# Joint gated norms, two banks for the turned chunks, two banks for the keys' products

## The chip, the cores and the metric

The kernel runs on one core of a Trainium2 chip. The core has five engines that run side by side and are ordered only by semaphores: TensorE (matrix products, results into the accumulator memory PSUM), VectorE, ScalarE, GpSimd and SyncE, which here issues the transfers. The metric is the device time of one execution in microseconds; lower is better. All data are float32. A product of two float32 matrices of full precision is made of three products of split operands (high by high, high by low, low by high), the lines L191 to L193.

## The reference, cut to what matters

One layer of a diffusion backbone over 1024 latent tokens and 256 context tokens, width 1024: a token mixer and then a convolutional channel mixer. The change lies in the token mixer, in its gated-DeltaNet heads (4 heads of 128):

```python
def bidir_gdn(q, k, v, beta, g, s0_f, s0_b):
    o_f, s_f = gated_delta_chunked(q, k, v, beta[:, :, 0], g[:, :, 0], s0_f)
    o_b, s_b = gated_delta_chunked(flip(q), flip(k), flip(v), flip(beta[:, :, 1]), flip(g[:, :, 1]), s0_b)
    return o_f + flip(o_b), s_f, s_b
...
kb = kc * bc[..., None]
a_mat = jnp.where(strict, jnp.einsum('nbhid,nbhjd->nbhij', kb, kc) * decay, 0.0)
t_inv = lax.linalg.triangular_solve(eye + a_mat, ...)   # per chunk and head
...
def mixer_out(u, o, z, w_f, g_gdn_l, w_out_l):
    y_f = fourier_mix(u, w_f)
    y_d = rmsnorm(o, g_gdn_l) * jax.nn.silu(z).reshape(...)
    return jnp.concatenate([y_f, y_d.reshape(bsz, length, V_W)], axis=-1) @ w_out_l
```

So each chunk needs the keys' products with themselves (`kc` with `kc`), times a decay, inverted; two scans run over the chunks in opposite directions; their sum is normalised per token and head (the norm), multiplied by a gate (gated norm), and goes with the Fourier part through the output projection.

## The kernel before, in words

Tokens are cut into ten tiles of 128: two of context, eight latent ones. The program is written as generators that are interleaved by hand (`both` alternates several, `drive` puts projection work between the yields of a main chain); a scheduler then lays out each engine's instructions in one fixed order. In a run each engine works through its own order and waits at its head.

The chain goes by batches of tiles. `decays` makes, per tile and direction, a decay matrix: two small rows are turned (L925), cast by ScalarE (L927), spread by GpSimd (L929, the tile `rh`), multiplied on TensorE (L953, L954) and exponentiated by ScalarE (L955). Once per tile, for both directions, TensorE makes the keys' products (L943, four heads) in the bank `sb`; VectorE multiplies them by the decay (L956), once per direction. Between them `lanes` of the batch before runs on VectorE: 31 steps of a product and a subtraction (L983, L985) on all triangles at once. Its result goes through DRAM (L988, L990), GpSimd masks it (L1007), and TensorE uses it (`finish`, L1013). Beside it TensorE has projections (L191 to L193) with convolutions on VectorE (L716 to L718, L735 on ScalarE).

Then ten scan steps follow, each on a pair of tiles, one per direction (`scan_step`). GpSimd scales a copy of the keys (L1102, `kd`), TensorE's products are all recorded at L1082, and VectorE updates the state (L1144) and the output (L1131, L1150). In the steps 6 to 9 both tiles of a step are finished for both directions (`seen`). Then each is normalised (`gdn_scale`): squares and sums on ScalarE (L1164), eight small instructions of VectorE on 128x4 values, among them the reciprocal square root of L201 to L206 (its root, L202, is ScalarE's), and four scalings of 128x128 on VectorE (L1170). One step later `gdn_out` turns each with four transposes (L1180) into a bank of the tag `a`, of which there is one; VectorE multiplies by the gate (L1182), ScalarE casts (L1189) and GpSimd takes the low part (L165). L165 is a helper: all subtractions for split operands carry that line. The banks have tags: `mm` has two, `g` three, `a` one, `sf` and `sb` one each; the scan uses `sf` and `sb` for its two directions.

The projection of the mixer's output runs over two groups of four tiles, in two halves of columns (`first_half`, `second_half`). It needs the turned chunks and the Fourier pages, which `load_yf` brings from DRAM (cast at L1204, split at L165). The norm behind it is L1365 and L1366. From about 660 us on the channel mixer runs; the change does not touch it.

Of the kernel before, what the change touches and what calls it, by code (L numbers as in the profile page):

```python
# [9 lines left out]
F32 = mybir.dt.float32  # L10
F32R = mybir.dt.float32r
BF16 = mybir.dt.bfloat16
AF = mybir.ActivationFunctionType
ALU = mybir.AluOpType
# [4 lines left out]
P = 128  # L19
# [5 lines left out]
NTC = CTX // P  # L25
NTA = NT + NTC
H = 4
# [73 lines left out]
class Kern:  # L101
# [802 lines left out]
    def decays(self, B):  # L904

        nc, kp, tiles = self.nc, self.kp, B["tiles"]
        V = nc.vector
# [28 lines left out]
        for u, (ti, t, d) in enumerate(units):  # L936
            st, rh = nxt
            if u + 1 < nu:
                nxt = rows(*units[u + 1][1:])
            if d == 0:  # L940
                kk = self.psum("sb")
                for h in range(H):
                    nc.tensor.matmul(kk[:, h * P:(h + 1) * P], self.kchunk(h, t), self.kchunk(h, t),  # L943
                                     start=True, stop=True, skip_group_check=True)
                W2 = self.pg().rearrange("p (d h n) -> p d h n", d=2, h=H)
                if t >= NTC:
                    EP = self.pg()
                    E2 = EP[:, 0:512], EP[:, 512:]
            W = W2[:, d]
            W = W.rearrange("p h n -> p (h n)")  # L950
            e = E2[d] if t >= NTC else W
            ps = self.psum("g")
            nc.tensor.matmul(ps, self.negm[:, d], self.idb.rearrange("p h n -> p (h n)"), start=True, stop=False)  # L953
            nc.tensor.matmul(ps, st[:, 0], rh.rearrange("p h n -> p (h n)"), start=False, stop=True)  # L954
            nc.scalar.activation(e, ps, AF.Exp)  # L955
            V.tensor_tensor(W, kk, e, op=ALU.mult)  # L956
            W = W2[:, d]
            for b in range(4):
                s = slice(32 * b, 32 * b + 32)
                (V.transpose if d == 0 else nc.scalar.copy)(CB[s, u], W[s, :, s])  # L960
            if d:
                nc.sync.dma_start(B["dw"][ti], W2.rearrange("p d h n -> p d (h n)"))
                if t >= NTC:
                    nc.sync.dma_start(self.Ed[t], EP.rearrange("p (d n) -> p d n", d=2))
            yield 1
# [97 lines left out]
    def scan_step(self, si):  # L1063

        nc = self.nc
        V = nc.vector
# [6 lines left out]
        R, vt, E, kd, vs, qs, o = ([None, None] for _ in range(7))  # L1073
        S = self.S
        T = self.steps[si]
# [14 lines left out]
        for d in range(2):  # L1090
            t = T[d]
# [54 lines left out]
        if lat:  # L1146
            for d in range(2):
                av = self.psum("g")
                mm(av, lambda h: E[d][:, hs(h)], lambda h: vs[d][:, hs(h)])
                V.tensor_tensor(o[d], o[d], av, op=ALU.add)  # L1150
            if seen:
                for d in range(2):
                    self.gdn_scale(T[d] - NTC)
        yield 1

    def gdn_scale(self, lt):

        nc, sp = self.nc, self.kp
        V = nc.vector
        o = self.o[lt]  # L1160
        ss = sp.tile([P, 2, H], F32, tag="oss", bufs=2, name=self.nm("oss"))
        s = self.sq[:, lt]
        for h in range(H):
            nc.scalar.activation(self.junk[:, :P], o[:, h * P:(h + 1) * P], AF.Square, accum_out=ss[:, 0, h:h + 1])  # L1164
        V.tensor_tensor(ss[:, 0], ss[:, 0], s, op=ALU.mult)
        V.tensor_tensor(ss[:, 0], ss[:, 0], s, op=ALU.mult)
        self.rsqrt(ss[:, 1], ss[:, 0], 1.0 / P, sp)
        V.tensor_tensor(ss[:, 1], ss[:, 1], s, op=ALU.mult)
        for h in range(H):
            V.tensor_scalar_mul(o[:, h * P:(h + 1) * P], o[:, h * P:(h + 1) * P], ss[:, 1, h:h + 1])  # L1170

    def gdn_out(self, lt):

        nc = self.nc
        o = self.o[lt]
        z = self.pg()[:, 0:512].rearrange("p (h n) -> p h n", h=H)
        nc.sync.dma_start(z, self.zs[:, :, lt * P:(lt + 1) * P].rearrange("h p n -> p h n"))
        ps = self.psum("a")
        for h in range(H):
            nc.tensor.transpose(ps[:, h * P:(h + 1) * P], o[:, h * P:(h + 1) * P], self.ident)  # L1180
        zf = z.rearrange("p h n -> p (h n)")
        nc.vector.scalar_tensor_tensor(zf, ps, self.gg, zf, op0=ALU.mult, op1=ALU.mult)  # L1182
        g, c0 = GCOL[lt]
        if self.yT[g][4] is None:
            self.yT[g][4:] = [self.page2() for _ in range(4)]
        for h in range(H):
            y = self.yT[g][4 + h]
            c = slice(c0, c0 + P)
            nc.scalar.copy(y[:, 0, c], z[:, h])  # L1189
            self.sub_l(nc.gpsimd, y[:, 1, c], z[:, h], y[:, 0, c])  # L1190
# [16 lines left out]
    def mixer(self):  # L1207
# [6 lines left out]
        with tc.tile_pool(name="mix", bufs=1, reuse_waits="tile") as kp:  # L1214
# [30 lines left out]
            for si in range(6, 10):  # L1245
# [6 lines left out]
                next(g)  # L1252
                if si >= 8:
                    next(h00)
                for lt in late:
                    self.gdn_out(lt)
                if si == 11:
                    self.load_yf(1)
                if si == 10:
# [15 lines left out]
            h10 = self.second_half(0, gp)  # L1275
            for _ in range(2):
                next(h10)
            for lt in late:
                self.gdn_out(lt)
            if 11 == 11:  # L1280
                self.load_yf(1)
            x0, self.h0w = [], []
# [590 lines left out]
```

## Time and profile before

| | |
|---|---|
| three runs | 1362.92, 1364.43, 1364.84 us (median 1364.43) |
| profiled execution | 1366.19 us, its span 1364.4 |
| TensorE busy | 1285.0 us (94% of the span) |
| VectorE busy | 992.6 us (73%) |
| ScalarE, GpSimd busy | 641.1 us (47%), 472.2 us (35%) |
| chain that ended last | TensorE 56%, VectorE 22%, DMA 8%, issue 5%, ScalarE 5% |

Busy shares are means over stages with different limits. In the rows below PE is TensorE's products, PEld its weight loads, DVE VectorE, ACT ScalarE, POOL GpSimd. "idle before <-releaser" is how long the engine stood still before an instruction and what it waited for. PEclk is the share of TensorE's full clock that was granted, as a mean over the window. One product of float32 shows as several records on TensorE, so four of them read "x8".

### The profile page before, as it was taken

The numbers are of one execution on the slowest core, as the hardware profiler recorded it, in microseconds if no ns is written. First come the engines' busy times: TensorE is split into PE (matmuls) and PEld (weight loads), VectorE is DVE, ScalarE is ACT, GpSimd is POOL, SyncE is SP. The second block draws the span as 40 slices with busy tenths as digits, with TensorE's granted clock in tenths as the row PEclk, the third lists the DMA queues.
The fourth block names the chain that finished last, engine by engine and source line by source line (L and its number), as shares of the span: only waits on it lengthen the run. The fifth ranks groups of instructions, "written<-read, shape, count | busy, mean of one in ns | idle before, by whom it ended". The sixth has DMA issues, their size and how long they took to land.

```text
span 1364.4 us, 19307 instructions
## 1 busy us (share of the span) xinstructions
PE 1285.0 (94%) x6678; PEld 1025.0 (75%) x6678; DVE 992.6 (73%) x1802; ACT 641.1 (47%) x1334; POOL 472.2 (35%) x464
## 2 busy tenths in 40 slices
PE   5999999989899999898999899999999999999994
PEld 2677886667557789786777688888888887888873
DVE  2465555944963856857469899888888889878997
ACT  5553456532554233444757444444444445555342
POOL 0221114332434252542126667665666650000000
PEclk9999999999999999999999899999999999999997
DMA  9622226676476778825432233332233166645665
GB/s 333 179 107 71 74 77 193 209 220 209 150 201 236 273 229 275 269 64 172 163 131 79 77 94 93 93 93 66 59 92 93 47 208 231 201 137 165 201 216 185
DMA packets 183732, 213.67 MB, mean 157 GB/s; under 512 B 31640, under 2 KB 119762, under 8 KB 183634
## 3 DMA queue, kind: packets, MB, share of 16 engines
q1 hardware_dynamic: 182769, 209.28, 47.8%
q0 software_dynamic: 864, 3.15, 0.7%
q8 instruction: 53, 0.87, 0.3%
q14 instruction: 46, 0.37, 0.1%
HBM read 163.11 MB, written 49.28 MB: 156 GB/s over the span
## 4 chain that ended last, share of the span: by engine, by line
PE 56%; DVE 22%; DMA 8%; issue 5%; ACT 5%; POOL 2%; SPq 1%; DVEq 0%; POOLq 0%; ACTq 0%
PE ps L191 14%; PE ps L193 14%; PE ps L192 14%; DVE cv L1472 4%; PE ps L1082 3%; DVE T L983 2%; DVE pg L985 2%; PE ps L305 2%; PE ps L1026 2%; DVE pg L1449 1%; DVE wl L165 1%; DVE pg L165 1%; PE ps L1013 1%; DVE s L1449 1%; DMA pg<-in_x_dram 1%
## 5 line engine op out<-in xcount | busy, mean ns | idle before, releaser
L191 PE MATMUL ps<-pg,wh 128*128 128x512 f32 (+1 forms) x896 | 351.7, 393 | 7.6 <-DVE pad L1449 5.2
L192 PE MATMUL ps<-pg,wh 128*128 128x512 f32 (+1 forms) x896 | 346.2, 386 | 0.0
L193 PE MATMUL ps<-pg,wl 128*128 128x512 f32 (+1 forms) x896 | 346.2, 387 | 0.0
L1472 DVE SCALAR_TENSOR_TENSOR cv<-pad,dw,cv 128x1024 f32<-128x1024 f32 x176 | 226.3, 1286 | 11.6 <-ACT cv L1470 8.2
L191 PEld LDWEIGHTS ps<-pg,wh 128*128 128x128 f32 x896 | 169.8, 190 | 56.1 <-issue 20.7
L193 PEld LDWEIGHTS ps<-pg,wl 128*128 128x128 f32 x896 | 169.7, 189 | 35.7 <-issue 3.5
L192 PEld LDWEIGHTS ps<-pg,wh 128*128 128x128 f32 x896 | 170.2, 190 | 30.9 <-issue 0.4
L165 POOL TENSOR_TENSOR wl<-wr,wh 128x512 fp32r<-128x512 f32 x68 | 89.4, 1322 | 188.7 <-ACT wh L183 158.0
L165 POOL TENSOR_TENSOR wl<-s,wh 128x512 fp32r<-128x512 f32 x80 | 107.7, 1349 | 62.2 <-ACT wh L1651 61.9
L1651 ACT CAST wh<-s 128x512 fp32r<-128x512 f32 x80 | 49.6, 621 | 120.1 <-PE ps L192 116.0
L191 PE MATMUL ps<-pg,pg 128*128 128x512 f32 (+1 forms) x248 | 98.5, 399 | 3.3 <-ACT pg L1616 1.8
L191 PE MATMUL ps<-wh,pg 128*128 128x512 f32 x250 | 97.8, 393 | 2.0 <-ACT pg L1616 1.7
L192 PE MATMUL ps<-pg,pg 128*128 128x512 f32 (+1 forms) x248 | 97.5, 395 | 1.0 <-POOL pg L165 0.7
L193 PE MATMUL ps<-pg,pg 128*128 128x512 f32 (+1 forms) x248 | 96.8, 395 | 1.4 <-DVE pg L355 0.8
L192 PE MATMUL ps<-wl,pg 128*128 128x512 f32 x250 | 97.6, 390 | 0.0
L193 PE MATMUL ps<-wh,pg 128*128 128x512 f32 x250 | 97.3, 390 | 0.0
L1082 PE MATMUL ps<-pg,pg 128*128 128x128 f32 x464 | 58.4, 277 | 0.7 <-ACT pg L1142 0.6
L191 PEld LDWEIGHTS ps<-pg,pg 128*128 128x128 f32 x248 | 47.7, 192 | 14.9 <-ACT pg L1616 2.2
L193 PEld LDWEIGHTS ps<-pg,pg 128*128 128x128 f32 x248 | 47.5, 193 | 13.8 <-issue 1.7
L1082 PEld LDWEIGHTS ps<-pg,pg 128*128 128x128 f32 x464 | 54.9, 192 | 2.7 <-ACT pg L1142 1.0
L192 PEld LDWEIGHTS ps<-pg,pg 128*128 128x128 f32 x248 | 47.8, 193 | 11.2 <-POOL pg L165 1.1
L191 PEld LDWEIGHTS ps<-wh,pg 128*128 128x128 f32 x250 | 46.9, 188 | 12.3 <-ACT pg L1616 2.1
(363 smaller groups left out, 2434.5 us busy)
## 6 DMA issues: line engine op xcount, KB each, us to landing
pg<-in_w_down_dram SPq DMA_DIRECT2D x97, 256.0 KB, 4.5
wr<-in_w_ada_dram SPq DMA_DIRECT2D x32, 512.0 KB, 4.5
wr<-in_w_up_dram SPq DMA_DIRECT2D x24, 512.0 KB, 3.8
wr<-in_w_in_dram SPq DMA_DIRECT2D x20, 512.0 KB, 4.3
pg<-in_w_up_dram SPq DMA_DIRECT2D x20, 512.0 KB, 5.4
wr<-in_w_down_dram SPq DMA_DIRECT2D x35, 256.0 KB, 2.7
gd<-pg SPq DMA_DIRECT2D x17, 512.0 KB, 2.7
pg<-gd SPq DMA_DIRECT2D x34, 256.0 KB, 4.6
```

Source lines behind the costliest of these rows:

```text
L165: eng.tensor_tensor(l, full, h.bitcast(F32), op=ALU.subtract)
L191: nc.tensor.matmul(out, ah, bh, start=start, stop=False, **kw)
L192: nc.tensor.matmul(out, ah, bl, start=False, stop=False, **kw)
L193: nc.tensor.matmul(out, al, bh, start=False, stop=stop, **kw)
L305: nc.tensor.matmul(ps[32 * j:32 * j + 32, :], self.csil[:, k, :], t[:, a, :], start=(k < 4), stop=(k >= 4), skip_group_check=True, tile_po ...
L983: V.tensor_tensor(tmp, L[:nl, j + 1:, j:j + 1].broadcast_to([nl, r, c]), X[:nl, j:j + 1, 0:c].broadcast_to([nl, r, c]), op=ALU.mult)
L985: V.tensor_tensor(X[:nl, j + 1:, 0:c], X[:nl, j + 1:, 0:c], tmp, op=ALU.subtract)
L1026: nc.tensor.matmul(ps[po, h * n:(h + 1) * n], Q[k0:k0 + kn, d, h, po], R[k0:k0 + kn, d, h, c0:c0 + n], start=True, stop=True, skip_group_c ...
L1082: nc.tensor.matmul(ps[:, hs(h)], lhs(h), rhs(h), start=True, stop=True, skip_group_check=True)
L1449: eng.tensor_tensor(o, a, b, op=op)
L1472: V.scalar_tensor_tensor(c3, src, w, c3, op0=ALU.mult, op1=ALU.add)
L1651: nc.scalar.copy(h, src)
```

## The change

Three edits, and the order that the scheduler makes of them. (1) In `decays` the keys' products go to `sb` and `sf` in turn, by the tile's place in its batch. (2) `gdn_scale` takes both tiles of a step: the small instructions are made once, on 128x8 values in place of 128x4 twice, and the scaling of each tile is one VectorE multiply of 128x512 with the factors broadcast over each head's 128 columns (L1173), in place of four of 128x128. The squares on ScalarE stay eight. (3) `gdn_out` takes a tag: the second tile of a step is turned in a bank of `g`. Behind the edited functions the line numbers are three higher: L1180 is L1183, L1182 is L1185.

```diff
--- before.py
+++ after.py
@@ -938,7 +938,7 @@
             if u + 1 < nu:
                 nxt = rows(*units[u + 1][1:])
             if d == 0:
-                kk = self.psum("sb")
+                kk = self.psum(("sb", "sf")[ti % 2])
                 for h in range(H):
                     nc.tensor.matmul(kk[:, h * P:(h + 1) * P], self.kchunk(h, t), self.kchunk(h, t),
                                      start=True, stop=True, skip_group_check=True)
@@ -1149,33 +1149,36 @@
                 mm(av, lambda h: E[d][:, hs(h)], lambda h: vs[d][:, hs(h)])
                 V.tensor_tensor(o[d], o[d], av, op=ALU.add)
             if seen:
-                for d in range(2):
-                    self.gdn_scale(T[d] - NTC)
+                self.gdn_scale([t - NTC for t in T])
         yield 1
 
-    def gdn_scale(self, lt):
+    def gdn_scale(self, lts):
 
         nc, sp = self.nc, self.kp
         V = nc.vector
-        o = self.o[lt]
-        ss = sp.tile([P, 2, H], F32, tag="oss", bufs=2, name=self.nm("oss"))
-        s = self.sq[:, lt]
-        for h in range(H):
-            nc.scalar.activation(self.junk[:, :P], o[:, h * P:(h + 1) * P], AF.Square, accum_out=ss[:, 0, h:h + 1])
+        lts = sorted(lts)
+        ss = sp.tile([P, 2, 2, H], F32, tag="oss", bufs=2, name=self.nm("oss"))
+        s = self.sq[:, lts[0]:lts[1] + 1:lts[1] - lts[0]]
+        for i, lt in enumerate(lts):
+            for h in range(H):
+                nc.scalar.activation(self.junk[:, :P], self.o[lt][:, h * P:(h + 1) * P], AF.Square,
+                                     accum_out=ss[:, 0, i, h:h + 1])
         V.tensor_tensor(ss[:, 0], ss[:, 0], s, op=ALU.mult)
         V.tensor_tensor(ss[:, 0], ss[:, 0], s, op=ALU.mult)
-        self.rsqrt(ss[:, 1], ss[:, 0], 1.0 / P, sp)
+        flat = lambda x: x.rearrange("p a h -> p (a h)")
+        self.rsqrt(flat(ss[:, 1]), flat(ss[:, 0]), 1.0 / P, sp)
         V.tensor_tensor(ss[:, 1], ss[:, 1], s, op=ALU.mult)
-        for h in range(H):
-            V.tensor_scalar_mul(o[:, h * P:(h + 1) * P], o[:, h * P:(h + 1) * P], ss[:, 1, h:h + 1])
-
-    def gdn_out(self, lt):
+        for i, lt in enumerate(lts):
+            o = self.o[lt].rearrange("p (h n) -> p h n", h=H)
+            V.tensor_tensor(o, o, ss[:, 1, i].unsqueeze(2).broadcast_to([P, H, P]), op=ALU.mult)
+
+    def gdn_out(self, lt, tag="a"):
 
         nc = self.nc
         o = self.o[lt]
         z = self.pg()[:, 0:512].rearrange("p (h n) -> p h n", h=H)
         nc.sync.dma_start(z, self.zs[:, :, lt * P:(lt + 1) * P].rearrange("h p n -> p h n"))
-        ps = self.psum("a")
+        ps = self.psum(tag)
         for h in range(H):
             nc.tensor.transpose(ps[:, h * P:(h + 1) * P], o[:, h * P:(h + 1) * P], self.ident)
         zf = z.rearrange("p h n -> p (h n)")
@@ -1252,8 +1255,8 @@
                 next(g)
                 if si >= 8:
                     next(h00)
-                for lt in late:
-                    self.gdn_out(lt)
+                for lt, tag in zip(late, "ag"):
+                    self.gdn_out(lt, tag)
                 if si == 11:
                     self.load_yf(1)
                 if si == 10:
@@ -1275,8 +1278,8 @@
             h10 = self.second_half(0, gp)
             for _ in range(2):
                 next(h10)
-            for lt in late:
-                self.gdn_out(lt)
+            for lt, tag in zip(late, "ag"):
+                self.gdn_out(lt, tag)
             if 11 == 11:
                 self.load_yf(1)
             x0, self.h0w = [], []
```

Three places where the order of an engine moves.

VectorE in `decays`, the second multiply of a tile by its decay (L956, `pg_3211`) among the steps of `lanes`. Before:

```order
L985 TENSOR_TENSOR pg_3091<-pg_3091,T_3094 128x22x10
L983 TENSOR_TENSOR T_3094<-pg_3089,pg_3091 128x231
L985 TENSOR_TENSOR pg_3091<-pg_3091,T_3094 128x21x11
L983 TENSOR_TENSOR T_3094<-pg_3089,pg_3091 128x240
L956 TENSOR_TENSOR pg_3211<-ps_3206,pg_3212 128x512
L985 TENSOR_TENSOR pg_3091<-pg_3091,T_3094 128x20x12
L983 TENSOR_TENSOR T_3094<-pg_3089,pg_3091 128x247
```

Now:

```order
L985 TENSOR_TENSOR pg_3091<-pg_3091,T_3094 128x22x10
L983 TENSOR_TENSOR T_3094<-pg_3089,pg_3091 128x231
L956 TENSOR_TENSOR pg_3211<-ps_3206,pg_3212 128x512
L985 TENSOR_TENSOR pg_3091<-pg_3091,T_3094 128x21x11
L983 TENSOR_TENSOR T_3094<-pg_3089,pg_3091 128x240
L985 TENSOR_TENSOR pg_3091<-pg_3091,T_3094 128x20x12
L983 TENSOR_TENSOR T_3094<-pg_3089,pg_3091 128x247
```

The multiply stands ahead of the subtraction `21x11` and the product after it, where it stood behind them.

GpSimd in scan step 6: the two key scalings (L1102) and the low parts of a weight (L165 of 128x1024). Before:

```order
L1102 TENSOR_TENSOR pg_5165<-pg_5165,dks 128x512
L165 TENSOR_TENSOR pg_5201<-wr_5198,pg_5200 128x1024
L1102 TENSOR_TENSOR pg_5172<-pg_5172,dks 128x512
L165 TENSOR_TENSOR pg_5207<-wr_5204,pg_5206 128x1024
L165 TENSOR_TENSOR pg_5236<-pg_5228,pg_5236 128x128
```

Now (the tiles are numbered anew):

```order
L1102 TENSOR_TENSOR pg_5148<-pg_5148,dks 128x512
L165 TENSOR_TENSOR pg_5184<-wr_5181,pg_5183 128x1024
L165 TENSOR_TENSOR pg_5190<-wr_5187,pg_5189 128x1024
L1102 TENSOR_TENSOR pg_5155<-pg_5155,dks 128x512
L165 TENSOR_TENSOR pg_5219<-pg_5211,pg_5219 128x128
```

The second key scaling has moved behind the second L165.

TensorE in the last part of the mixer: the transposes of step 9's two chunks, the first and the second, each with the products next to it. Before:

```order
L192 MATMUL ps_5858<-pg_5797,pg_5239 128x512
L193 MATMUL ps_5858<-pg_5796,pg_5239 128x512
L1180 MATMUL ps_5912<-cst,pg_4149 128x128 x4
L191 MATMUL ps_5968<-pg_5778,pg_5027 128x512
L192 MATMUL ps_5968<-pg_5779,pg_5027 128x512
```

and 33 rows further on:

```order
L191 MATMUL ps_6022<-pg_5784,pg_5037 128x512
L192 MATMUL ps_6022<-pg_5785,pg_5037 128x512
L1180 MATMUL ps_5928<-cst,pg_4149 128x128 x4
L193 MATMUL ps_6022<-pg_5784,pg_5037 128x512
L191 MATMUL ps_6022<-pg_5784,pg_5042 128x512
```

Now:

```order
L192 MATMUL ps_5790<-pg_5729,pg_5222 128x512
L193 MATMUL ps_5790<-pg_5728,pg_5222 128x512
L1183 MATMUL ps_5844<-cst,pg_4149 128x128 x4
L1183 MATMUL ps_5860<-cst,pg_4149 128x128 x4
L191 MATMUL ps_5900<-pg_5710,pg_5027 128x512
L192 MATMUL ps_5900<-pg_5711,pg_5027 128x512
```

Both chunks' transposes stand together, where 32 projection products lay between them.

## Rows read from the trace of the kernel before

**Rows 1.** Windows: span, busy per engine (count), PEclk, DMA, GB/s

```profile
400.00:545.00 145.00, 144.17 (x1179) 120.00 (x1178) 87.40 (x219) 51.17 (x130) 56.28 (x52) 1.00 0.77 252
...
660.00:1364.00 704.00, 671.25 (x2950) 550.95 (x2948) 592.80 (x806) 332.65 (x575) 271.57 (x202) 0.98 0.41 131
```

**Rows 2.** Waits of TensorE, 340 to 400: total, times, longest

```profile
PE ps L943 <- DVE pg L956: 5.2, 2, 3.1
```

**Rows 3.** Windows of 10 us, same columns

```profile
360.00:370.00 10.00, 10.00 (x36) 7.01 (x36) 9.46 (x17) 7.35 (x12) 5.10 (x8) 0.83 0.38 139
370.00:380.00 10.00, 7.98 (x32) 5.13 (x31) 8.71 (x20) 4.36 (x19) 2.00 (x2) 0.83 0.24 95
...
560.00:570.00 10.00, 7.24 (x43) 6.57 (x42) 9.53 (x31) 1.96 (x7) 5.11 (x7) 0.83 0.74 233
...
630.00:640.00 10.00, 7.65 (x29) 6.23 (x30) 7.40 (x18) 5.34 (x18) 6.37 (x10) 0.83 0.55 185
```

**Rows 4.** Timeline: start, us, instruction, [idle before, releaser], 355 to 359

```profile
355.01 2.34 DVE L985 TENSOR_TENSOR pg<-pg,T 128x231 f32<-128x231 f32 x1
...
355.84 1.25 POOL L165 TENSOR_TENSOR wl<-wr,wh 128x512 fp32r<-128x512 f32 x1
...
357.72 0.68 DVE L956 TENSOR_TENSOR pg<-ps,pg 128x512 f32<-128x512 f32 x1
...
358.45 1.16 PE L943 MATMUL ps<-pg 128*128 128x128 f32 x8 [3.15 <-DVE pg L956]
```

**Rows 5.** Timeline of TensorE, second wait

```profile
373.47 1.89 PE L943 MATMUL ps<-pg 128*128 128x128 f32 x8 [2.02 <-DVE pg L956]
```

**Rows 6.** Timeline, 365 to 370, the next decay products

```profile
366.63 0.35 ACT L927 CAST st<-ps 64x256 fp32r<-64x256 f32 x1
...
367.06 1.08 POOL L929 TENSOR_TENSOR rh<-st,cst 64x512 fp32r<-64x512 f32 x1 [1.25 <-ACT st L927]
...
368.91 0.42 DVE L983 TENSOR_TENSOR T<-pg,pg 128x255 f32<-128x255 f32 x1
...
368.92 0.49 PE L954 MATMUL ps<-rh,st 64*128 64x512 f32 x1
```

**Rows 7.** Timeline of VectorE, inversion's second half and end

```profile
385.80 0.48 DVE L716 TENSOR_SCALAR pg<-pg,cw 128x513 f32<-128x513 f32 x1 [2.07 <-ACT pg L735]
...
394.29 0.19 DVE L985 TENSOR_TENSOR pg<-pg,T 128x31 f32<-128x31 f32 x1
```

**Rows 8.** Timeline, GpSimd and TensorE before L1013

```profile
408.96 2.08 POOL L1007 TENSOR_TENSOR pg<-ct,cst 128x512 f32<-128x512 f32 x2
...
413.62 0.60 PE L1013 MATMUL ps<-pg,pg 128*128 128x128 f32 x4
```

**Rows 9.** Lines of VectorE, whole span: count, busy, mean ns, idle

```profile
L1366 DVE TENSOR_TENSOR pg<-pg,pg 128x512 f32<-128x512 f32 x16 | 10.7, 710 | 0.0
...
L1170 DVE TENSOR_SCALAR pg<-pg,oss 128x128 f32<-128x128 f32 x32 | 7.7, 305 | 0.1
```

**Rows 10.** Timeline, 560 to 565, step 6

```profile
560.37 1.04 POOL L1102 TENSOR_TENSOR pg<-pg,dks 128x512 f32<-128x512 f32 x1
...
561.37 2.33 POOL L165 TENSOR_TENSOR pg<-wr,pg 128x1024 fp32r<-128x1024 f32 x1
...
561.46 2.26 DVE L206 SCALAR_TENSOR_TENSOR oss<-rsq,oss 128x4 f32<-128x4 f32 x1
...
564.30 0.52 PE L1180 MATMUL ps<-cst,pg 128*128 128x128 f32 x2 [2.76 <-DVE pg L1170]
```

**Rows 11.** Timelines of TensorE, ScalarE, GpSimd around step 9's transposes

```profile
632.35 0.66 PE L1180 MATMUL ps<-cst,pg 128*128 128x128 f32 x4 [4.31 <-DVE pg L1182]
...
638.11 0.39 PE L191 MATMUL ps<-wh,pg 128*128 128x512 f32 x1
...
637.12 0.67 ACT L1204 CAST pg<-yft 128x512 fp32r<-128x512 f32 x1 [0.80 <-DMA yft<-yf]
...
636.94 2.57 POOL L165 TENSOR_TENSOR pg<-yft,pg 128x512 fp32r<-128x512 f32 x2
```

## The prediction

> **What bounds the kernel now.** I read the windows by stage first, because the change touches only the stages up to 660 us: the instruction order of everything behind it is the same in both programs. TensorE is the bound behind it, at 671.25 us busy of 704, and in the scan stretch from 400 to 545 us, at 144.17 of 145 [rows 1]; there the reader is to see that a microsecond which TensorE gains earlier can be kept, since nothing else sets the pace. The stretch from 340 to 400 (decays and a triangular inversion on VectorE) is not like that. Then the list of TensorE's waits: in that stretch it waits for VectorE's L956 at L943, 5.2 us in two waits [rows 2]. Then the windows by granted clock: four stretches of 10 us run at a mean of 0.83 of full clock, and each lies at one of the waits that the change addresses [rows 3]. A mean of 0.83 over 10 us is 0.17 x 10 = 1.7 us of full-clock work that such a stretch lacks, where TensorE is busy. Last the timelines around the waits.
>
> **Part A: the keys' products alternate between two banks.** Nothing is added: the same matmuls and multiplies. Before, the four products of the next key tile wait at the head of TensorE until L956 has read the previous tile's bank. The first wait is 3.15 us: L956 (0.68) starts at 357.72, behind an L985 of 2.34 us that runs beside GpSimd's L165 [rows 4]. The second wait is 2.02 us [rows 5]. With two banks the previous reader of the bank is a whole tile back, so both waits go. In the new order L956 also stands ahead of that L985. Sum at TensorE: 3.15 + 2.02 = 5.2 us, and if the low clock behind both goes too, 2 x 1.7 = 3.4 more, 8.6 in all.
>
> What is late next? Two places. First, the product with `rh` (L954) at 368.92 needs GpSimd's L929, which ends at 367.06 + 1.08 = 368.14 and follows ScalarE's L927 at 366.63 [rows 6]; the slack is 0.78 us. That chain starts from VectorE and moves with it: L956 ends at 358.40 before, and at about 355.7 if it stands ahead of the 2.34 us, 2.7 earlier. So the first wait's gain is held to about 2.7 + 0.8 = 3.5 of its 3.15 + 1.7 = 4.85. Second, the inversion's last instruction ends at 394.48 on VectorE [rows 7]; a round trip through DRAM and the eight GpSimd multiplies L1007 (the last pair of them 408.96 + 2.08 = 411.04) lead to TensorE's L1013 at 413.62 [rows 8], slack 2.58. VectorE had idle time of its own there that comes from TensorE being late (2.07 us at 385.80 before L716, for ScalarE's copy of a matmul's result [rows 7]); with that and the 2.7 above, it can end 2 to 4.8 earlier, so L1013 allows 4.6 to 7.4. From both sides: A gives at most 8.6, and at least the second wait plus nothing for the first, 2.0. I take 5.5: 3.5 for the first place and 2.0 for the second, whose clock I don't count, as another wait may keep it low.
>
> **Part B: the joint norm, steps 6 to 9.** It removes per step eight scalings on VectorE (L1170, 32 in four steps, 305 ns each [rows 9]), 8 x 0.305 = 2.44 us, and one of two sets of small instructions; it adds two broadcast multiplies of 128x512 with both inputs in SBUF. The nearest row is L1366, 128x512 with both inputs in SBUF, 710 ns [rows 9]: 1.42 us. VectorE saves about a microsecond in each step, beside the small set. It decides nothing, except at step 6. There TensorE waits 2.76 us at 564.30 for the first tile's scaling, behind an L206 of 2.26 us that is stretched beside GpSimd's L165 of 2.33 [rows 10]. In the new order that transpose stands later on TensorE and doesn't wait. But the order moves GpSimd's second key scaling (L1102) behind the second L165, and its products (L1082) in front of the transposes on TensorE. That scaling then ends at 560.37 + 2.33 + 1.04 = 563.74, where it ended at 561.41; TensorE has by 561.53 no work left ahead of it and waits some 2.2 to 2.6 us. One wait of 2.76 becomes one of about 2.5: nothing gained, between +2 (if the multiplies are stretched also) and -2 (if the chain lets GpSimd begin earlier). I take 0.
>
> This very multiply doesn't stand in the trace. L983 is one with broadcast inputs, half as long: 0.42 us for 128x255 with GpSimd idle [rows 6], so the broadcast seems to cost nothing and two such are 0.84. From above, a two-input instruction beside GpSimd's work took 2.34 (L985 [rows 4]). I take 0.71, as GpSimd has nothing left when the multiplies come (after 563.74).
> The Trainium skill (SBUF — State Buffer, section "Who interferes with whom") has a VectorE instruction with two SBUF inputs and a GpSimd instruction that reads SBUF exclude each other for a whole instruction, whichever comes second waiting. The stretched L985 and L206 agree with it. By that rule both new multiplies could each be held for one of GpSimd's instructions; the sum of part B would then be up to 3.3 us worse (an estimate), and with GpSimd idle it would stay as it is.
>
> **Part C: finished chunks turn in two banks.** Before, the second chunk's transposes wait for the first chunk's L1182 to read the only bank: 4.31 us at 632.35, since L1182 stands behind other VectorE work [rows 11]. Behind it lies one of the four stretches at 0.83 [rows 3]: 1.7 us. Both go, 4.31 + 1.7 = 6.0. What is late next is near: Some matmuls later TensorE begins the next group's projection, at 638.11 before and 6.0 earlier, about 632, now. It needs the Fourier pages, whose last arrives by DMA for ScalarE's L1204 at 637.12, and two subtractions of GpSimd from 636.94 to 639.51 [rows 11]. These stand behind this chunk's own L165 on GpSimd, which the new bank lets start earlier; then each follows its L1204 at once, and I put the two pages at 637.3 and at 637.12 + 0.67 + 1.29 = 639.1 at the latest, 638.6 with a little gained. The wait of 4.31 turns into one of some 4 us. Bounds: -4 (the pages come early) and +1. I take -1.
>
> Sum: -5.5 + 0 - 1 = -6.5. Against the profiled execution, 1366.19, that is 1359.7. The profiled execution lies 1.76 above the median of 1364.43, so against the median it is 1357.9.
>
> **Rivals.**
> 1. The whole gain: all the waits and the clock behind them go. 8.6 (A) + 6.0 (C) + 2.76 and a clock window of 1.7 (B) = 19; with half of B and C given back some 14 to 15, which is 1350. For it: four separate clock windows that sit at exactly these waits. Against it: each has a follower within a few microseconds [rows 6, 8, 11].
> 2. No change (within 0.2%, about 2.7 us, is what a measurement of this kernel can't tell from none): VectorE sets the pace of the inversion, so L1013 waits for what TensorE gained, and the Fourier pages take C. A gives 2.0, B and C nothing: 1362.4. For it: the slack is only 2.58 us and VectorE is nearly full until 395. Against it: VectorE's own wait of 2.07 us is TensorE's delay, and goes with it.
> 3. Slower: the key scaling of step 6 is late (behind the second L165), the step's state update follows it, and the broadcast multiplies come beside GpSimd's work. Each costs up to 2.34 - 0.71 = 1.6 beyond its price; with 2.3 for the late L1102, and 1.7 for a clock that falls again, that is +7.2 in step 6. It decides if A keeps less than 4: 1364.4 - 2.0 + 7.2 = 1369.6 at worst, 1368.0 with one multiply stretched. For it: L206 and L985 were stretched so [rows 4, 10]. Against it: in the new order TensorE goes on with matmuls there, and the transposes no longer head the queue.
> 4. The banks change nothing, because the "sf" bank has another reader in the stretch. The scan, its other user, doesn't run from 340 to 400. I give it no time of its own; it is in case 2.
>
> **How the numbers follow.** Forecast (A carried for 3.5 to 7.4, B and C near nothing): 0.50, 1354 to 1361.5. Rival 1: 0.18, 1346 to 1353. Rival 2, with 4: 0.19. Rival 3: 0.13. The range leaves out the outer half of rival 1 and of rival 3: 1349 to 1366. Faster by over 0.2%: forecast and rival 1, 0.68. Same: rival 2 and 0.02 of rival 3, where A keeps more, 0.21. Slower: 0.11.
>
> **What would show it.** A right: no wait for L956 at L943 in the trace of after; full clock from 360 to 380; L1013 earlier by 4 to 7 us, with or without a wait of its own. A wrong: L943 gone from the waits, but L954 or L1013 waits for GpSimd for as long. B: in step 6 a wait at L1082 for GpSimd's L1102 of 2 to 3 us, and L1173 about 0.7 us each; wrong if L1173 takes 2 us. C: no wait at L1183 for L1185, and a new one at the next group's L191 to L193 for Fourier pages. The forecast as a whole is wrong if the start of the channel mixer comes less than 3 or more than 11 us earlier than before.

## The result and the profile after

The change makes the kernel slower by half a per cent: 1371.11 us median (1368.34 to 1376.92, 7 runs) against 1364.15 us (1362.75 to 1366.23, 7 runs), a ratio of 1.0055, interval 1.0036 to 1.0073. A second measurement gave 1.0039 (1.0024 to 1.0053; experiment e4). The forecast was 1357.9.

The execution that was profiled took 1376.92 us, span 1375.1, and is the slowest of the seven. Part of its excess is not the change's, as the first windows below show. First the windows by stage of the kernel after (span, busy per engine with counts, PEclk, DMA share, GB/s), which answer to [rows 1, 3], and then the 60 us from 340 to 400 of the kernel before.

```profile
300.00:310.00 10.00, 10.00 (x60) 4.55 (x60) 3.26 (x6) 2.02 (x3) 0.81 (x1) 0.54 0.16 51
310.00:320.00 10.00, 10.00 (x71) 6.43 (x67) 2.21 (x4) 2.26 (x5) 0.00 (x0) 0.61 0.37 128
340.00:400.00 60.00, 50.63 (x237) 32.56 (x241) 49.34 (x108) 28.55 (x76) 18.71 (x27) 0.91 0.41 141
360.00:370.00 10.00, 9.55 (x47) 6.62 (x46) 9.34 (x15) 6.22 (x23) 5.88 (x8) 1.00 0.34 122
370.00:380.00 10.00, 8.05 (x37) 5.53 (x36) 9.77 (x15) 6.45 (x10) 5.89 (x8) 1.00 0.39 138
380.00:390.00 10.00, 5.44 (x14) 2.09 (x12) 9.00 (x21) 3.69 (x15) 1.26 (x1) 0.66 0.15 59
400.00:545.00 145.00, 143.22 (x1120) 115.49 (x1119) 85.40 (x213) 52.14 (x128) 56.69 (x53) 1.00 0.76 241
...
650.00:660.00 10.00, 8.23 (x31) 6.36 (x31) 7.17 (x20) 3.56 (x11) 2.69 (x3) 0.83 0.26 106
674.00:1375.00 701.00, 668.75 (x2947) 548.73 (x2945) 590.44 (x806) 333.11 (x574) 269.95 (x202) 0.99 0.41 131
```

```profile
340.00:400.00 60.00, 54.35 (x238) 34.37 (x235) 49.76 (x105) 31.25 (x82) 18.52 (x23) 0.94 0.50 163
```

The two clock windows at 0.83 between 360 and 380 us are gone, as forecast. In their place one at 0.66 stands right behind, and in it TensorE is busy for 5.44 us of 10. Behind 674 us TensorE's row is as full as it was. The windows from 300 to 320 lack (1 - 0.54) x 10 + (1 - 0.61) x 10 = 8.5 us of full-clock work. The kernel before has full clock there, and so has e1, with the same bank edit; the same kernel profiled once more (e4) has 0.89 and 1.00. One with the bank edit in the last batch alone (e5), whose order in these windows is that of the kernel before, shows 0.51 and 0.64. I put this stretch down to the single run, and don't reason from the absolute times of this trace, but from intervals inside it.

TensorE's waits of the kernel after, 340 to 400 us (total, times, longest), answer to [rows 2]:

```profile
PE ps L866 <- ACT sqj L867: 4.6, 1, 4.6
PE ps L1082 <- DVE pg L1109: 2.2, 1, 2.2
PE ps L954 <- POOL rh L929: 1.6, 2, 0.8
PE ps L953 <- ACT st L927: 0.7, 2, 0.5
PE ps L305 <- DMA wr<-in_w_ada_dram: 0.4, 1, 0.4
```

The 5.2 us at L943 are gone. L866 (transposes of the queries), L954 and L953 wait in its place, 6.9 us together. The 2.2 us at L1082 belong to a scan step that ends before 340 us in the kernel before, with 1.4 us of the same wait there. The timeline of the kernel after around the longest of these waits (start, duration, instruction, [idle before, releaser]):

```profile
364.52 2.35 DVE L983 TENSOR_TENSOR T<-pg,pg 128x231 f32<-128x231 f32 x1
366.80 0.68 DVE L956 TENSOR_TENSOR pg<-ps,pg 128x512 f32<-128x512 f32 x1
...
381.85 0.68 DVE L956 TENSOR_TENSOR pg<-ps,pg 128x512 f32<-128x512 f32 x1
...
382.57 1.22 ACT L960 COPY pg<-pg 32x128 f32<-32x128 f32 x4 [3.86 <-DVE pg L956]
383.81 0.60 ACT L955 ACTIVATE pg<-ps 128x512 f32<-128x512 f32 x1
384.30 0.27 ACT L867 ACTIVATE sqj<-ps 128x128 bf16<-128x128 f32 x1
...
384.84 0.48 PE L866 MATMUL ps<-cst,pg 128*128 128x128 f32 x1 [4.56 <-ACT sqj L867]
...
395.49 0.49 DVE L716 TENSOR_SCALAR pg<-pg,cw 128x513 f32<-128x513 f32 x1 [1.67 <-ACT pg L735]
...
405.32 0.19 DVE L985 TENSOR_TENSOR pg<-pg,T 128x31 f32<-128x31 f32 x1
407.09 0.69 DVE L956 TENSOR_TENSOR pg<-ps,pg 128x512 f32<-128x512 f32 x1 [1.57 <-ACT pg L955]
...
413.94 1.05 POOL L1007 TENSOR_TENSOR pg<-pg,cst 128x512 f32<-128x512 f32 x1 [9.21 <-issue]
...
423.67 3.29 PE L1013 MATMUL ps<-pg,pg 128*128 128x128 f32 x28
```

Read from the end: TensorE's transpose at 384.84 waits for ScalarE's square L867, which frees its bank. The square stands behind four copies L960 and an L955 in ScalarE's order. The copies wait for VectorE's L956 at 381.85, the very instruction for which L943's second wait stood before. TensorE no longer waits for L956 itself, but for something queued behind it.

Step 6 of the scan in the kernel after, answering to [rows 10], and step 9's follower, answering to [rows 11]:

```profile
573.03 2.27 DVE L1167 TENSOR_TENSOR oss<-oss,sq__3830 128x8 f32<-128x8 f32 x1
...
577.62 1.29 DVE L1173 TENSOR_TENSOR pg<-pg,oss 128x512 f32<-128x512 f32 x2
...
570.58 4.70 POOL L165 TENSOR_TENSOR pg<-wr,pg 128x1024 fp32r<-128x1024 f32 x2
575.22 1.05 POOL L1102 TENSOR_TENSOR pg<-pg,dks 128x512 f32<-128x512 f32 x1
...
576.33 1.22 PE L1082 MATMUL ps<-pg 128*128 128x128 f32 x8 [2.23 <-POOL pg L1102]
...
648.38 0.50 PE L191 MATMUL ps<-wh,pg 128*128 128x512 f32 x1 [0.45 <-ACT pg L1207]
...
651.48 0.51 PE L193 MATMUL ps<-wh,pg 128*128 128x512 f32 x1 [2.37 <-POOL pg L165]
...
652.74 0.79 PE L193 MATMUL ps<-wh,pg 128*128 128x512 f32 x1 [0.29 <-POOL pg L165]
```

Both forecast followers are there: TensorE waits 2.23 us for the late key scaling L1102, and 0.45 + 2.37 + 0.29 = 3.1 us for the Fourier pages. The new multiply costs 688 ns. The line of VectorE, whole span (count, busy, mean ns, idle before):

```profile
L1173 DVE TENSOR_TENSOR pg<-pg,oss 128x512 f32<-128x512 f32 x8 | 5.2, 688 | 0.1
```

### The profile page after: what moved, and what is told of

Same layout as the page of the kernel before. It is cut to its first block, busy times and chain, and to the rows that moved or that the text cites. A ratio compares the mean times of both kernels' runs of the same rounds, so it can differ in the third digit from the quotient of the medians.

```text
span 1375.1 us, 19251 instructions
## 1 busy us (share of the span) xinstructions
PE 1291.0 (94%) x6673; PEld 1025.8 (75%) x6678; DVE 983.3 (72%) x1746; ACT 640.5 (47%) x1330; POOL 472.5 (34%) x464
## 4 chain that ended last, share of the span: by engine, by line
PE 33%; DVE 13%; issue 6%; DMA 4%; POOL 3%; ACT 3%; SPq 0%; DVEq 0%; POOLq 0%; ACTq 0%
PE ps L191 10%; PE ps L193 9%; PE ps L192 9%; DVE cv L1475 4%; PE ps L1082 2%; DVE pg L1452 1%; POOL pg L165 1%; DVE s L1452 1%; DVE wl L165 1%; DVE pg L165 1%; DVE pad L1616 1%; PE cv L193 1%; POOL wl L165 1%; PE cv L192 1%; PE cv L191 1%
## 5 line engine op out<-in xcount | busy, mean ns | idle before, releaser
L192 PE MATMUL ps<-pg,wh 128*128 128x512 f32 (+1 forms) x896 | 346.3, 386 | 0.0
L192 PEld LDWEIGHTS ps<-pg,wh 128*128 128x128 f32 x896 | 169.6, 189 | 32.4 <-issue 2.2
L165 POOL TENSOR_TENSOR wl<-wr,wh 128x512 fp32r<-128x512 f32 x68 | 89.9, 1331 | 180.2 <-ACT wh L183 152.5
L165 POOL TENSOR_TENSOR wl<-s,wh 128x512 fp32r<-128x512 f32 x80 | 107.1, 1341 | 61.8 <-ACT wh L1654 61.5
L192 PE MATMUL ps<-pg,pg 128*128 128x512 f32 (+1 forms) x248 | 97.4, 395 | 3.0 <-POOL pg L165 2.8
L192 PE MATMUL ps<-wl,pg 128*128 128x512 f32 x250 | 97.8, 391 | 0.0
L1082 PE MATMUL ps<-pg,pg 128*128 128x128 f32 x464 | 58.7, 277 | 0.0
L191 PEld LDWEIGHTS ps<-pg,pg 128*128 128x128 f32 x248 | 47.6, 192 | 13.7 <-ACT pg L1619 1.4
L193 PEld LDWEIGHTS ps<-pg,pg 128*128 128x128 f32 x248 | 47.0, 191 | 14.3 <-DVE pg L355 1.9
L192 PEld LDWEIGHTS ps<-pg,pg 128*128 128x128 f32 x248 | 47.6, 192 | 13.4 <-POOL pg L165 3.6
L193 PEld LDWEIGHTS ps<-wh,pg 128*128 128x128 f32 x250 | 47.4, 190 | 13.0 <-POOL pg L165 3.5
L191 PEld LDWEIGHTS ps<-wh,pg 128*128 128x128 f32 x250 | 47.4, 190 | 12.5 <-ACT pg L1619 2.2
```

What stands on the lines that cost most here:

```text
L165: eng.tensor_tensor(l, full, h.bitcast(F32), op=ALU.subtract)
L191: nc.tensor.matmul(out, ah, bh, start=start, stop=False, **kw)
L192: nc.tensor.matmul(out, ah, bl, start=False, stop=False, **kw)
L193: nc.tensor.matmul(out, al, bh, start=False, stop=stop, **kw)
L1082: nc.tensor.matmul(ps[:, hs(h)], lhs(h), rhs(h), start=True, stop=True, skip_group_check=True)
```

## Experiments

The kernel before was run beside each set. Ratios are to it, with a 95% interval. A, B and C are the parts of the prediction: keys' products in two banks, joint norm, turn in two banks.

**e1 to e4: the parts alone.** e1 is A alone (`kk = self.psum(("sb", "sf")[ti % 2])`), e2 the change without that line, e3 the tags of `gdn_out` alone, e4 the whole change again.

> Only the keys' products alternate between two banks; norms and turned chunks as before. Theory 1 (the bank edit costs it, by the order that it gives TensorE: the products of the first finished tiles lose the projection work that lay between them, and TensorE runs at the low clock from 300 to 318 us): 5 to 9 us slower than before, 1369 to 1373, the shift already there at 345 us. Theory 2 (step 6 costs it, with the late key scaling): 1360 to 1364, not slower than before.

> The joint norms and the two turning banks without the bank edit of the keys' products. Theory 1: 1364 to 1367, 0 to 3 us slower (the 3 us that the trace of the changed kernel loses in step 6). Theory 2: 1369 to 1372, all of the loss.

> Only the second tile's turn in a bank of its own. Both theories: within 2 us of before; the wait of 4.3 us for L1182 gone, and a wait for the Fourier pages of some 4 us in its place.

> The changed kernel as it is, once more. Theory 1: 1369 to 1373. Whether the low clock from 300 to 318 us of its first trace comes again is open: if it does, it belongs to the order; if the time stays and the clock doesn't fall, the loss lies in the waits.

Before had 1367.01 us here. e1: 1371.92, ratio 1.0039 (1.0026 to 1.0052). e2: 1365.98, 1.0000 (0.9984 to 1.0017). e3: 1370.94, 1.0029 (1.0013 to 1.0046). e4: 1372.19, 1.0039 (1.0024 to 1.0053). e1 alone loses as much as e4, and e2 nothing that can be told: the loss is part A's, the part from which the gain was forecast. e1 came out just under the 5 to 9 us of its first theory, but not by its mechanism, as its clock from 300 to 320 us is full. C alone loses 3.9 us where both theories had it within 2, and B with C doesn't: the parts don't add. In e3's trace TensorE waits three times in step 6 and behind it for the old scalings L1170 (4.4 us in all, before 2.8); in e2, with the joint norm, it waits 0.2 for L1173.

e1 also shows a wait that I had not put in the sum. TensorE's waits from 255 to 275 us, before and then e1 (total, times, longest):

```profile
PE ps L824 <- DVE pg L956: 0.7, 1, 0.7
```

```profile
PE ps L824 <- DVE pg L956: 3.0, 1, 3.0
```

L824 turns the values in a bank of tag `sb`, which holds a keys' product of another batch. With the banks alternating, the L956 that frees it is a later one: 2.3 us more of waiting. That it costs time isn't shown: the scan's first product (L1082) stands at 321.83 us in e1 and at 321.40 before.

**e5, e6: the bank in the last batch alone, and ScalarE's order.** e5 leaves the earlier batches alone; e6 adds that ScalarE's copies of tile 7 stay behind the first square of the group that the transposes wait for.

```diff
-                kk = self.psum("sb")
+                kk = self.psum(("sb", "sf")[ti % 2] if tiles[0] == 4 else "sb")
```
```diff
+                        if (h, t0, i) == (1, 0, 0):
+                            for c in self.copies[7]:
+                                self.tc.add_manual_dep(c, a.ins.name, ..., reason="order")
```

> Two banks for the keys' products in the last batch of tiles only (340 to 400 us, where the prediction saw its waits), one bank before it. Theory 1 (each new wait belongs to a place: the turned values share the bank sb with the first batches' products, the squares L867 stand behind copies that wait for L956): the wait at L824 for L956 falls from 3.0 to about 0.7 us, the 4.56 us at L866 for L867 stays; 1 to 3 us faster than with all batches, so 1 to 4 us slower than before. Theory 2 (what TensorE gains in this stretch it gives back at whatever comes next): as slow as with all batches, 5 us.

> As the run before, and ScalarE's order held at one place: the first square of the second q head (L867) issues before the four copies of the decay blocks that wait for VectorE's L956. Theory 1: no wait of 4.56 us at L866, full clock from 380 to 390, and the gain that was forecast for the bank edit appears in part: 3 to 6 us faster than the run before, 0 to 4 us faster than before. Theory 2: the wait goes to the next place (L953, L954, L1013), and the time stays within 1.5 us of the run before.

Before 1364.89. e5: 1368.64, 1.0027 (1.0012 to 1.0041); its L824 waits 0.7 as before, so that wait needs the earlier batches' banks. e6: 1366.59, 1.0013 (0.9997 to 1.0029). The wait at L866 falls from 4.3 us to 3.1 and is still one for a square: now the second. Holding one square moves the wait to the next. e5 came out as its first theory said, but its trace doesn't show where it loses: from the second L956 of the last batch to the first L1365 it takes 260.6 us, before 261.8. What this execution has more than that of before lies ahead of 345 us, with the low clock from 300 to 320. e6 lies between its two theories, 2 us below e5, and the intervals overlap.

**e7, e8: GpSimd's order in step 6.** e7 is e2 with the weight's L165 held behind the second key scaling; e8 is e6 with that and with B and C.

```diff
-            self.sub_l(nc.gpsimd, l, raw, h)
+            with self.tc.issue_after(self.kds.ins):
+                self.sub_l(nc.gpsimd, l, raw, h)
```

> Joint norms and two turning banks, one bank for the keys' products, and GpSimd's order held at one place: both key scalings (L1102) of the step issue before the weights' low parts (L165). Theory of the forecast's part B (the late scaling makes the wait of 2.3 us at L1082 in step 6): that wait goes, 1 to 3 us faster than without the hold, so 0 to 4 us faster than before. Rival (the wait turns into one for the next product or for the transposes): within 1 us of the kernel without the hold.

> All three edits, the bank edit in the last batch only, with both holds. Theory 1: 2 to 7 us faster than before. Theory 2 and the rival of the run before: as before within 2 us, or slower.

e7: 1368.11, 1.0028 (1.0016 to 1.0041). e8: 1367.16, 1.0015 (0.9998 to 1.0032). TensorE's waits in e7, 550 to 575 us:

```profile
PE ps L1183 <- DVE pg L1173: 2.6, 1, 2.6
PE ps L1082 <- DVE pg L1109: 0.5, 1, 0.5
PE ps L1082 <- POOL pg L1102: 0.2, 1, 0.2
```

With the scaling in time, the transposes wait 2.6 us for the new multiply instead. So e7, forecast to be faster, is slower than before, and than e2, which is the same without the hold (1.0000). e8 shows no gain either, as its second theory said. Around step 6 TensorE's longest wait is 2.0 to 2.9 us in every version that was run, mostly for one or the other of two things that are late together.

**e9 to e11: all four squares held, the whole change with it, and B alone.** e9 is e6 with `(1, 0, 3)` in place of `(1, 0, 0)`; e10 adds B and C; e11 is B alone.

> Two banks in the last batch only, and all four squares (L867) of the second q head's first bank before the copies that wait for VectorE's L956; with only the first square held, the wait at L866 fell just from 4.3 to 3.1 us. Theory 1 (ScalarE's order is what eats the gain): no wait over 0.5 us at L866, L1013 starts at 408 to 410 where it was at 413.6, 2 to 5 us faster than before. Theory 2 (VectorE's inversion paces the stretch; L956 comes at the same time whatever TensorE does): L956 stays at its times within 1 us of before, the wait shows up at the next products (L953, L954) or at L1013, and the time is that of before within 2 us.

> All three edits with the bank edit in the last batch only and the four squares held, GpSimd's order as the scheduler makes it. Theory 1: 2 to 5 us faster than before. Theory 2: as before within 2 us.

> Only the joint norms. Norms and turn together were as before, the turn alone 4 us slower. If the two edits simply add, the norms alone are 3 to 5 us faster than before; if the turn alone lost by the order that it gave step 6, which the joint norms undo, the norms alone are within 2 us of before, with a wait of about 2.3 us at L1082 for the late key scaling and the wait of 4.3 us for L1182 kept.

Before 1367.85. e9: 1368.49, 1.0009 (0.9991 to 1.0027). e10: 1369.28, 1.0015 (0.9996 to 1.0033). e11: 1367.48, 1.0003 (0.9985 to 1.0020). In e9 L866 waits no longer. Its waits of TensorE, 340 to 420 us (line numbers are one to five higher here: L320 is L319, L310 is L309):

```profile
PE ps L320 <- DVE adaev L310: 3.2, 1, 3.2
PE ps L306 <- DMA wr<-in_w_ada_dram: 1.5, 3, 0.7
PE ps L959 <- POOL rh L934: 0.8, 1, 0.8
PE ps L958 <- ACT st L932: 0.8, 1, 0.8
```

The third instruction in turn waits some 3 us for VectorE, here a plain copy. Behind it stands a window of low clock, and in it VectorE waits for ScalarE (L992 is the L985 of before, L961 its L956, L960 its L955):

```profile
391.22 0.68 DVE L310 COPY adaev<-ps 128x512 f32<-128x512 f32 x1
391.95 1.87 PE L320 MATMUL ps<-cst,adaev 128*128 128x1 f32 x8 [3.20 <-DVE adaev L310]
392.28 0.19 DVE L992 TENSOR_TENSOR pg<-pg,T 128x31 f32<-128x31 f32 x1
...
398.69 0.69 DVE L961 TENSOR_TENSOR pg<-ps,pg 128x512 f32<-128x512 f32 x1 [4.47 <-ACT pg L960]
```
```profile
390.00:400.00 10.00, 8.05 (x27) 5.99 (x28) 3.97 (x11) 1.71 (x5) 1.22 (x1) 0.66 0.81 174
```

e9 and e10 came out as their second theories said, without a gain, and e11 as its second. From e5 to e9 the ratio falls by 0.0018, but the intervals overlap; that ScalarE's order costs something with two banks is not shown by the times.

**e12 to e14: less work for VectorE.** e12 is the kernel before without the subtractions L985 of the middle batch's inversion, which runs in this stretch. e13 leaves out its products L983 too, and e14 is e13 with e5's bank line. None of the three makes the inverses of that batch.

```diff
-            V.tensor_tensor(tmp, L[...], X[...], op=ALU.mult)
-            V.tensor_tensor(X[...], X[...], tmp, op=ALU.subtract)
+            if B["tiles"][0] != 2:
+                V.tensor_tensor(tmp, L[...], X[...], op=ALU.mult)
+                V.tensor_tensor(X[...], X[...], tmp, op=ALU.subtract)
```

> The kernel before, with one bank for the products as before, and with less work for VectorE: the subtractions of the inversion (L985) are left out for the middle batch, the one that is inverted beside the last batch's products, so the results differ from the reference. Theory 'VectorE sets the pace from 345 to 395 us': with some 4 to 8 us of VectorE's work gone, the masks of L956 come earlier, both waits at L943 (3.15 and 2.02 us) fall under 1 us though no bank was added, the front sum of L1013 stands at 405 to 409 us instead of 413.62, and the time is 4 to 8 us below that of before. Theory 'the one bank and ScalarE's order set the pace': the waits at L943 still sum to 4 us or more, L1013 stays within 2 us of its place, and the time is within 2 us of before.

> The kernel before, one bank, with the inversion's 62 vector instructions (L983, L985) left out for the middle batch alone, so the results differ from the reference; about 31 us of VectorE's 49.8 us between 340 and 400 go. Theory 'VectorE sets the pace there': the first wait at L943 (3.15 us for L956) falls under 1 us, the second too, the front sum of L1013 stands 5 to 9 us earlier than in the kernel before, and the time is 4 to 9 us below it (1358 to 1363 where before has 1367). Theory 'TensorE paces, its full row and the clock': TensorE was busy 54.4 of these 60 us, so at most those 5.6 us and the clock's 1.7 can come, and L1013 moves by under 3 us and the time by under 2.

> The same kernel with the two banks for the keys' products of the last batch (the bank edit of e5), the only other difference; against e13 it shows what the second bank is worth when VectorE is nearly free. Theory 'VectorE sets the pace': with its work gone the masks of L956 are on time, so the second bank is worth nothing more: within 2 us of e13, both below before. Theory 'ScalarE's order (copies of L960 ahead of the squares of L867) eats the gain': the wait at L866 for L867 stays at 3 us or more with the bank and the time is 3 us or more above e13. Theory 'the bank itself costs': slower than e13 by the 3.7 us that e5 lost against before, though VectorE is free.

e12: 1364.81 against 1367.02, 0.9996 (0.9978 to 1.0014). One of the two waits at L943 went, the other stayed at 3.4 us: the scheduler had put six of the remaining L983 ahead of L956, 7.14 us of them. It met neither expectation. Its trace takes 256.6 us from the second L956 to the first L1365, 5.2 less than before, but its eleven runs show no gain; why is open. e13: 1354.83 against 1365.11, 0.9933 (0.9912 to 0.9954). e14: 1355.05, 0.9917 (0.9889 to 0.9945). Windows of e13, then of e14, in the same columns as above:

```profile
340.00:400.00 60.00, 58.93 (x289) 37.94 (x290) 29.36 (x60) 34.98 (x95) 23.25 (x32) 1.00 0.62 179
```

```profile
340.00:400.00 60.00, 59.33 (x286) 38.67 (x285) 31.03 (x56) 38.02 (x102) 28.04 (x34) 1.00 0.71 206
```

and TensorE's waits in e13, the same 60 us:

```profile
PE ps L1083 <- DVE pg L1110: 1.2, 1, 1.2
PE ps L305 <- DMA wr<-in_w_ada_dram: 1.1, 2, 0.7
```

With one bank, as before, both waits at L943 are gone, the clock is full, and TensorE is busy 58.93 of 60 us (54.35 before, 50.63 with the change). The time is 9 us lower (0.67% of 1365.11). The second bank adds nothing that can be told from that: 1355.05 and 1354.83, and overlapping intervals (e14 has six runs, and its interval leaves some us either way). This is what the theory "VectorE sets the pace" expected, at its upper end. The other theories of these two runs fall: TensorE's full row allowed under 2 us, and a bank that costs by itself would have shown 3 us or more in e14. One reserve: the scheduler set the rest in another order too once the work was gone, so the 9 us are not VectorE's time alone.

Four intervals sum up the row of traces, each inside one execution (us; lines of the kernel before). I: from the second to the eighth L956 of the last batch. II: the inversion beside it, from its L985 of 128x207 to its last L985. III: from the same L985 to the L1013 that follows. IV: from the second L956 to the first L1365, some 260 us on; of what the three parts touch, only the last step's turn comes behind it.

| | I | II | III | IV |
|---|---|---|---|---|
| before | 40.1 | 42.9 | 62.3 | 261.8 |
| the change | 40.3 | 44.0 | 62.3 | 265.8 |
| e1 | 40.2 | 43.7 | 62.2 | 265.7 |
| e4, the change again | 40.2 | 43.8 | 62.3 | 265.4 |
| e5 | 40.4 | 44.5 | 62.6 | 260.6 |
| e8 | 38.3 | 42.2 | 60.4 | 262.5 |
| e9 | 40.7 | 40.7 | 62.9 | 262.6 |
| e2, no bank edit | 39.1 | 41.9 | 61.2 | 260.8 |
| e12 | 37.7 | | | 256.6 |
| e13 | 36.8 | | | 255.0 |
| e14 | 36.3 | | | 255.5 |

The second bank alone (e1, e5) leaves L1013 where it was, to 0.4 us (III). With the squares held (e9) the inversion ends 2.2 us earlier than before (II), and L1013 still doesn't: TensorE loses the time at L310's copy and at the low clock behind it. I is not VectorE's alone, since before the eighth L956 VectorE stands idle for ScalarE's L955, which follows TensorE's L954: 4.47 us in e9, and in the kernel before

```profile
397.81 0.69 DVE L956 TENSOR_TENSOR pg<-ps,pg 128x512 f32<-128x512 f32 x1 [2.65 <-ACT pg L955]
```

It is also shorter in e2 and e8, without a gain in time. By far the shortest IV are those of e12 to e14, which take work from VectorE.

## Why the prediction was wrong

**What bounds the kernel** was read rightly: TensorE's row is full from 400 to 545 us in both (143.22 of 145), and 340 to 400 is unlike it. The list of waits and the clock windows were also right about where TensorE stood still. One count is off, without effect: the row at 408.96 ends the seventh L1007, not the eighth.

**Part A failed**, and with it the forecast: -5.5 became about +5 (e1: 1.0039 of 1367). Its first half held: both waits at L943 went, and the clock from 360 to 380 came back to 1.00. The step that failed is "What is late next? Two places", in both places and in their number.

In the first, L956 was to come "2.7 earlier". Counted from the inversion's L985 of 128x207 (351.37 before, 361.32 with the change) the second L956 comes 5.5 us behind it, where it was 6.4: 0.9 earlier. The L985 of 2.34 us is no longer ahead of it, but the L983 before that one, 1.38 us before (353.60), now takes 2.35.

In the second, "VectorE had idle time of its own there that comes from TensorE being late ...; with that and the 2.7 above, it can end 2 to 4.8 earlier". Counted from the same L985, the inversion's last instruction comes 0.8 us later in e1 and 1.1 with the change (column II). VectorE was as busy as before, 49.34 us of the 60 against 49.76. Its idle time didn't go with the waits at L943 either: before L716 it is 1.67 us where it was 2.07 [rows 7], and 1.62 stand before the L956 at 390.90, behind ScalarE's L955, as 1.56 did before. GpSimd's chain L1007 follows the inversion's end as before, 8.6 us behind its last L985 (402.79, 8.5 us, before).

The third place I did not name. I had looked at what TensorE reads next and not at what else is queued behind L956: ScalarE's copies L960 and, behind them, the squares L867. TensorE's wait for them is 4.56 us, with 3.4 us of full-clock work lacking in the window behind it. rh's slack of 0.78 us did come up too (0.8, twice). The sign that I gave for A being wrong, a wait at L954 or L1013 as long as that at L943, didn't come: L954 has 1.6 us and L1013 none. Together the 3.5 and 2.0 of the sum became nothing (column III).

So rival 2, "VectorE sets the pace of the inversion", was right in what it put the stretch down to: e13 and e14 show it, with the reserve said there. Its wait at L1013 didn't come, and its time, 1362.4, was not right. It kept the second wait's 2.0 us as a gain, and had no loss in it. The trace of the kernel before could have told: the chain that ended last runs on VectorE's inversion and on ScalarE's L960 and L867 there, with L983 and L985 at 30% of it from 340 to 400 us (start, duration, what):

```profile
355.01 2.35 DVE pg L985
...
358.43 0.30 ACT pg L960
...
359.37 0.28 ACT sqj L867
...
361.29 2.41 DVE T L983
```

What makes the loss of some 5 us I leave open. In the traces some 3 us of it lie behind the stretch that I had reasoned about: from L1013 to the first L1365 it is 209.0 us with the change and in e1 and 208.6 in e4, where it was 205.9 before. But e5, with 204.4 there, loses too. In e1 and e4 TensorE waits about 2 us for L1144 near 480 us; but so does e3, without the bank edit, and the profiled run of the change doesn't. The longer wait at L824 and ScalarE's order are not shown to cost time.

The rule of the Trainium skill that speaks for this edit (Perfetto Trace Analysis, section "Matmuls") has independent groups of products rotate through the banks, so that the evacuation of one overlaps the next. The trace agrees on the wait, 5.2 us to none, and not on the time: 1.0039 in e1. By e13 and e14 the engine that evacuates was itself the pace.

**Part B was right** at step 6, in its mechanism and in its price. The wait of 2.76 [rows 10] became one of 2.23 at L1082 for L1102, where 2.2 to 2.6 was said. L1173 took 688 ns where 710 was taken, in all eight. e11 gives 1.0003. The stretched multiplies of rival 3 didn't come; what was stretched is one small L1167 of 2.27 us beside L165, off the path. This agrees with the rule of the Trainium skill that the prediction cites (SBUF — State Buffer, section "Who interferes with whom"): it hits who comes second, and GpSimd was done when the multiplies came. e7 shows that the scaling and the multiply are late together, so that the other order doesn't help.

**Part C was right in its mechanism.** The 4.31 us at the transposes went, and TensorE waits 3.1 us for the Fourier pages, where "some 4" was said, with one clock window at 0.83 again behind it. A second follower was not in the sum: with B and C together TensorE also waits 2.5 to 2.8 us at L192 for a weight's low part from GpSimd (the change, e2, e4), 0.7 before. B with C is 1.0000, so the term of -1 can't be told from 0. That C alone loses (e3) was not foreseen: I costed the parts as if they added, and with the joint norm the second bank is harmless.

**Rival 1** falls at each of its four places, since each had a follower. **Rival 4** falls too: the bank had no reader that TensorE waited for in this stretch. It was `sb`, the old bank, that had one, elsewhere.

## What to carry to other kernels

A wait of TensorE for a VectorE instruction was worth nothing here, since that instruction stood behind other work of VectorE: the second bank only let TensorE run on to the next thing that VectorE, or an engine queued behind it, delivered late. Before buying a bank, follow the chain that ended last through the stretch, and list what else is queued behind the late instruction, on every engine. Taking all of that work away from VectorE told it (e13); taking away half didn't (e12). And list all users of a bank's tag over the whole program, not only in the stretch that is to gain.

## What was not expected of the hardware

- The same 20 us of small products (32x32, L1026) and modulation rows ran at a granted clock of 0.54 and 0.61 in one execution of the change and of 0.51 and 0.64 in one of e5, and at 1.00 in that of the kernel before, with TensorE's row full in all three. What TensorE did before doesn't tell them apart: both low ones follow two waits at L1013 (1.52 and 1.76 us, 1.76 and 1.76), but e6 and e8 have two of 2.1 to 2.2 and 1.8 there and full clock behind them. The mean of one L1026 in these 20 us was 305 ns with the change against 221 before.
- A VectorE instruction on 128x8 values took 2.27 us (L1167) beside GpSimd's L165, where the other three L1167 took 0.17: even so small an instruction was held for a whole one of GpSimd (2.35).
- Freed time on VectorE was partly taken back: in e12 six of the remaining products L983 took 7.14 us, 1.2 each, beside 5 us of GpSimd's multiplies and subtractions (353.12 to 358.07), where one took 0.42 with GpSimd idle [rows 6].
